# Splitting the tail of a mixture-of-experts decoder by column halves on one Trainium2 core

## The chip, the cores and the metric

The program runs on one core of one Trainium2 chip. The metric is the device time of one execution in microseconds (us), as the median of a few runs. The engines, as the profile names them: PE is TensorE (matrix products, PEld its weight loads), DVE is VectorE, ACT is ScalarE, POOL is GpSimd, SP is SyncE, which issues the DMA transfers here. In the trace each engine's instructions start in the order in which they stand in the program, and an instruction that needs another engine's result waits for it on a semaphore.

## The reference

Two layers of a hybrid decoder work on 256 tokens of 1024 channels in float32. Only the end of the second layer matters here: eight experts, the result added to the residual stream `x`, and the last normalisation.

```
def swiglu(x, w_gate, w_up, w_down):
    return (jax.nn.silu(x @ w_gate) * (x @ w_up)) @ w_down
...
h = rms_norm(x) * (1 + sc2) + sh2
f = moe_ffn(h, ...)          # top 2 of 8 experts for each token, EXPERT_DIM 3584
x = x + g2 * f
...
return rms_norm(x, final_norm_w)   # x * rsqrt(mean(x*x) + EPS) * final_norm_w
```

## The kernel before

The residual stream is a tile `xs` of 128 partitions by two token tiles (t = 0, 1) by 1024 columns, and columns are treated in two halves of 512, called c = 0 and c = 1 here. Weights stream from memory once: SP loads 1 MB pieces into `raw` tiles, and for each half of a piece ACT makes a rounded copy `whi` (line 170) and DVE the rest `wlo = raw - whi` (line 172), so that a product of full precision is three products on PE (`mm3`: high by high, high by low, low by high; every `mm` has line 96). The `whi` and `wlo` tiles go round in a ring of four or five.

The experts run one after the other (`expert`). Each gathers its tokens, makes gate and up products, and then the down products: 14 pieces of `moe_w_down`, each with two blocks of rows (k), and for each block three products into the PSUM tile of c = 0 and three into that of c = 1. In the rows of the order below, `mmt_16767` is the PSUM tile of c = 0 of the last expert and `mmt_16768` that of c = 1; a `whi` and a `wlo` with following numbers are the two parts of one block. After the down products comes `outer` for the expert: DVE scales a half by the token weights and the gate (printed as line 1549, the line of the helper `behind`), ACT makes its rounded part `yh` (also line 1549), DVE the rest `yl`, shown as `sg` (line 1598), PE multiplies both by the transposed selection `PTm` into an `smt` tile for each token tile, and DVE adds it to `xs` (line 1607). For the first seven experts this is queued beside the gate and up products of the next one (`Stages`). After the last expert nothing follows it, so `stages.flush()` issues it at once, and then `finish` runs: ACT squares `xs` and sums it along the columns (`rms_scale`, line 266), DVE turns the sums into 1/sqrt with three Newton steps (`newton`, lines 112 to 123) for each token tile apart, POOL meanwhile multiplies `xs` by the final weight row `fw` (line 1354), and ACT (line 1360) and DVE (line 1358) multiply that by the root and SP writes four blocks of 256 KB to `out` (line 1361). The `overflow` loop behind it is there for experts with more than 128 tokens.

A scheduler places the recorded instructions of each engine. It may move an instruction forward past others that it does not depend on; `tc.issue_after(ins)` (and the helper `behind`, which takes the instruction from the table `last`) keeps what is recorded under it behind `ins` on the engine of `ins`, and nothing else does.

Of the kernel before, what the change touches and what calls it, by code (L numbers as in the profile page):

```python
# [19 lines left out]
P = 128  # L20
D = 1024
# [40 lines left out]
def trunk_kernel(ctx, tc, a, out, dbg=None):  # L62
# [32 lines left out]
    def mm(o, l, r, start, stop):  # L95
        return T.matmul(o, l, r, start=start, stop=stop, skip_group_check=True)  # L96

    def mm3(o, lh, ll, rh, rl, start, stop):
        mm(o, lh, rh, start, False)
        mm(o, lh, rl, False, False)  # L100
        mm(o, ll, rh, False, stop)

    nsm = [0]

# [1205 lines left out]
    def moe(l):  # L1310
        with tc.tile_pool(name=f"mw{l}", bufs=1, reuse_waits="tile", side="right") as xp, \
# [14 lines left out]
            with tc.tile_pool(name=f"mr{l}", bufs=1, reuse_waits="tile") as rp, \  # L1326
# [18 lines left out]
                def finish():  # L1345
# [3 lines left out]
                    o, f = (x.rearrange("p (t n) -> p t n", t=NT) for x in (o, f))  # L1349
                    for t in range(NT):  # L1350
                        rs = rms_scale(t, lambda c: o[:, t, c * 512:(c + 1) * 512])
# [3 lines left out]
                        for c in range(2):  # L1355
                            cs = slice(c * 512, (c + 1) * 512)
                            if c:
                                V.tensor_scalar(o[:, t, cs], f[:, t, cs], rs, None, op0=OP.mult)
                            else:
                                A.activation(o[:, t, cs], f[:, t, cs], AF.Copy, scale=rs)  # L1360
                            nc.sync.dma_start(out[t * P:(t + 1) * P, cs], o[:, t, cs])

                for e in range(NE):
                    x, Pm, i = ready.pop(0)

                    def between():
                        Pm = behind("lo", pair, e + 1)
                        ready.extend((x, Pm, i) for i, x in enumerate(gather(l, ep, h2, Pm, 2)))
                    expert(l, e, ep, xp, x, lambda t, Pm=Pm, i=i: Pm[:, t, i], lambda t, e=e: wsel[:, t, e:e + 1], g2,
                           after_first if e == 0 else None, between if e % 2 and e < NE - 1 else None)  # L1370
                stages.flush()
                finish()
                overflow(l, mp, ep, xp, h2, g2, ovi, ovs, finish)
            extra.clear()

# [175 lines left out]
    def expert(l, e, ep, xp, x, Pm, wsel, g2, after=None, between=None):  # L1551

# [23 lines left out]
        def weights():  # L1576
# [9 lines left out]
            V.tensor_copy(ws, pst[:, 256:257])  # L1586
            return PTm, ws

        def outer(pss):
            yield 2  # L1590
            yp = []
            for c in range(2):
                y = pss[c]
                behind("lo", V.scalar_tensor_tensor, y, y, ws, g2[c], op0=OP.mult, op1=OP.mult)
                yh = ep.tile([P, 512], F32R, name="yh", tag="yh", bufs=2)
                yl = ep.tile([P, 512], F32R, name="sg", tag="sg", bufs=3)
                behind("hi", A.activation, yh, y, AF.Copy)
                V.tensor_sub(yl, y, yh.bitcast(F32))
                yp.append((yh, yl))
            yield 1  # L1600
            for c in range(2):
                cs = slice(c * 512, (c + 1) * 512)
                for t in range(NT):
                    ps = smtile()
                    mm(ps, PTm[:, t * P:(t + 1) * P], yp[c][0], True, False)
                    mm(ps, PTm[:, t * P:(t + 1) * P], yp[c][1], False, True)
                    V.tensor_add(xs[:, t, cs], xs[:, t, cs], ps)

        for c in range(ED // 512):
            pss = []  # L1610
# [12 lines left out]
                PTm, ws = weights()  # L1623
        pss = [mmtile(), mmtile()]
        KE = ED // P
        for k0 in range(0, KE, 2):
            if k0 == KE - 6 and between is not None:
                between()
            hi, lo = chunk(moe_src("moe_w_down", e)[k0 // 2, 0], 2, D)
            for k in range(2):  # L1630
                kk = k0 + k
                o = kk // 4 % 2 * 1024 + kk % 4 * P
                for c in range(2):
                    cs = slice(c * 512, (c + 1) * 512)
                    a2 = act[kk // 8]
                    mm3(pss[c], a2[:, o:o + P], a2[:, o + 512:o + 512 + P], hi[k][:, cs], lo[k][:, cs], kk == 0,
                        kk == KE - 1)
            stages.run()
        stages.add(outer(pss))

    def overflow(l, mp, ep, xp, h2, g2, ovi, ovs, finish):

# [153 lines left out]
```

## Time and profile before

| | us |
|---|---|
| three runs | 1902.97, 1904.64, 1906.03 |
| their median | 1904.64 |
| the profiled execution | 1905.8 |
| its span, from the first to the last instruction | 1904.0 |
| PE busy in that span | 1847.7 |

Times inside the trace count from the start of the span. The profiled execution is 1.2 us over the median, and 1.8 us of it lie outside the span. A busy PE is the sum of its instructions' durations; products overlap, so the distance between starts tells the pace. In a timeline row the columns are the start, the time covered by the merged instructions, engine, line, operation, output and input, the number merged, and in brackets how long the engine was idle before and what ended that.

### The profile page before, as it was taken

Reading aid. Unit: us, or ns where it says so; the run is one execution under the profiler, and the core shown is the slowest. Engines: PE = TensorE matmul, PEld = TensorE weight load, DVE = VectorE, ACT = ScalarE, POOL = GpSimd, SP = SyncE. Lnnn points to the kernel's source line nnn. Section 1 sums busy time; section 2 is a strip of 40 time slices with the busy share of each in tenths; the row PEclk is TensorE's granted clock in tenths of the full one; section 3 lists DMA queues with packets and bytes.
Section 4 is the critical chain, followed back from the end, with each engine's and each line's share of the span. In section 5 each row is a group of like instructions: output and inputs, shape, how many; then the busy total and the mean of one; then the engine's idle time right before and its main releaser. Section 6 shows DMA issues by size and latency. Waiting matters only on the chain.

```text
span 1904.0 us, 25647 instructions
## 1 busy us (share of the span) xinstructions
PE 1847.7 (97%) x9490; PEld 1548.6 (81%) x9490; DVE 1598.7 (84%) x2313; ACT 1230.9 (65%) x1599; POOL 41.5 (2%) x61
## 2 busy tenths in 40 slices
PE   8989999999999999999999999999999999999996
PEld 6889888788879898888888777878878888788785
DVE  7988786876578987667999889998898999899997
ACT  4655445544455644446777787777777777777775
POOL 0000100000000000000000000000000000000001
PEclk9999999999999999999999999999999999999998
DMA  9463545676545555558899989999889999899892
GB/s 364 175 213 125 199 177 202 241 290 238 205 169 199 198 185 193 176 200 329 334 356 343 354 320 361 343 365 355 339 333 356 351 358 368 311 354 381 332 353 91
DMA packets 75016, 530.19 MB, mean 278 GB/s; under 512 B 8578, under 2 KB 8962, under 8 KB 12548
## 3 DMA queue, kind: packets, MB, share of 16 engines
q1 hardware_dynamic: 74884, 528.49, 73.6%
q8 instruction: 76, 1.25, 0.3%
q14 instruction: 56, 0.46, 0.1%
HBM read 527.41 MB, written 1.05 MB: 278 GB/s over the span
## 4 chain that ended last, share of the span: by engine, by line
PE 84%; DVE 8%; ACT 4%; DMA 2%; issue 2%; ACTq 0%; DVEq 0%; SPq 0%
PE mmt L96 74%; PE smt L96 5%; DVE wlo L172 2%; DMA raw<-in_w_in_dram 2%; PE sst L96 2%; PE trt L1566 1%; DVE raw L199 1%; ACT whi L170 1%; DVE cv L588 1%; ACT sg L1527 1%; PE trt L258 0%; PE trt L1073 0%; PE trt L96 0%; DMA raw<-in_ffn_w_up_dram 0%; ACT htmp L289 0%
## 5 line engine op out<-in xcount | busy, mean ns | idle before, releaser
L172 DVE TENSOR_TENSOR wlo<-raw,whi 128x1024 fp32r<-128x1024 f32 (+1 forms) x874 | 1041.9, 1221 | 151.7 <-ACT whi L170 131.6
L170 ACT ACTIVATE whi<-raw 128x1024 fp32r<-128x1024 f32 (+1 forms) x874 | 907.8, 1059 | 316.4 <-PE mmt L96 263.4
L96 PE MATMUL mmt<-whi,xx 128*128 128x512 f32 x1792 | 578.9, 397 | 0.0
L96 PEld LDWEIGHTS mmt<-whi,xx 128*128 128x128 f32 x1792 | 337.4, 188 | 74.9
L96 PE MATMUL mmt<-wlo,xx 128*128 128x512 f32 x896 | 357.6, 399 | 4.9 <-DVE wlo L172 4.9
L96 PE MATMUL mmt<-whi,act 128*128 128x512 f32 x896 | 281.0, 391 | 1.2 <-ACT whi L170 1.2
L96 PEld LDWEIGHTS mmt<-wlo,xx 128*128 128x128 f32 x896 | 168.8, 188 | 52.1 <-DVE wlo L172 16.5
L96 PEld LDWEIGHTS mmt<-whi,act 128*128 128x128 f32 x896 | 167.4, 188 | 36.4 <-ACT whi L170 2.5
L96 PE MATMUL mmt<-whi,hh 128*128 128x512 f32 (+2 forms) x480 | 183.9, 389 | 4.8 <-ACT hh L292 2.0
L96 PE MATMUL mmt<-wlo,hh 128*128 128x512 f32 (+2 forms) x480 | 180.9, 382 | 1.0 <-DVE wlo L172 1.0
L96 PE MATMUL mmt<-whi,hl 128*128 128x512 f32 (+2 forms) x480 | 180.8, 382 | 0.5 <-DVE hl L293 0.5
L96 PE MATMUL mmt<-wlo,act 128*128 128x512 f32 x448 | 175.2, 391 | 1.8 <-DVE wlo L172 1.6
L199 DVE CUSTOM_DVE_ANT_0 raw<-raw,sc_b,pv 128x1024 f32<-128x1024 f32 x96 | 121.7, 1281 | 7.9 <-DMA raw<-in_w_ada_gate_dram 4.7
L96 PEld LDWEIGHTS mmt<-whi,hh 128*128 128x128 f32 x480 | 90.7, 189 | 22.8 <-ACT hh L292 2.6
L96 PEld LDWEIGHTS mmt<-whi,hl 128*128 128x128 f32 x480 | 90.6, 189 | 18.0 <-DVE hl L293 1.0
L96 PEld LDWEIGHTS mmt<-wlo,hh 128*128 128x128 f32 x480 | 90.6, 189 | 17.4 <-DVE wlo L172 1.6
L96 PEld LDWEIGHTS mmt<-wlo,act 128*128 128x128 f32 x448 | 84.1, 188 | 22.3 <-DVE wlo L172 4.4
L96 PE MATMUL mmt<-hh,wlo 128*128 128x256 f32 x320 | 92.9, 292 | 4.4 <-DVE wlo L172 4.4
L96 PE MATMUL mmt<-hh,whi 128*128 128x256 f32 x320 | 93.4, 293 | 1.5 <-ACT whi L170 1.5
L96 PE MATMUL mmt<-hl,whi 128*128 128x256 f32 x320 | 92.1, 289 | 0.0
L1549 ACT ACTIVATE act<-trt 128x512 fp32r<-128x512 f32 x56 | 33.1, 591 | 72.0 <-PE trt L1566 72.0
L96 PEld LDWEIGHTS mmt<-hh,wlo 128*128 128x128 f32 x320 | 61.9, 194 | 6.0 <-DVE wlo L172 5.8
(422 smaller groups left out, 2209.6 us busy)
## 6 DMA issues: line engine op xcount, KB each, us to landing
raw<-in_moe_w_gate_dram SPq DMA_DIRECT2D x112, 1024.0 KB, 5.9
raw<-in_moe_w_up_dram SPq DMA_DIRECT2D x112, 1024.0 KB, 6.4
raw<-in_moe_w_down_dram SPq DMA_DIRECT2D x112, 1024.0 KB, 6.6
raw<-in_w_in_dram SPq DMA_DIRECT2D x50, 1024.0 KB, 4.9
raw<-in_w_ada_pair_dram SPq DMA_DIRECT2D x32, 1024.0 KB, 5.5
raw<-in_w_ada_gate_dram SPq DMA_DIRECT2D x16, 1024.0 KB, 4.9
raw<-in_ffn_w_down_dram SPq DMA_DIRECT2D x11, 1024.0 KB, 4.8
raw<-in_ffn_w_gate_dram SPq DMA_DIRECT2D x10, 1024.0 KB, 4.9
```

What stands on the lines that cost most here:

```text
L96: return T.matmul(o, l, r, start=start, stop=stop, skip_group_check=True)
L170: last["hi"] = A.activation(hi[:, :m], r, AF.Copy)
L172: last["lo"] = V.tensor_sub(lo[:, :m], r, hi[:, :m].bitcast(F32))
L199: last["ada"] = V.tensor_tensor_reduce(r, r, sc_b, 1.0, pv[l][:, PP_BADA + i:PP_BADA + i + 1], OP.mult, OP.add, modc[l][:, i:i + 1])
L588: V.scalar_tensor_tensor(cv[:, s:], o[:, :S - s], tapw(3 - s), cv[:, s:], op0=OP.mult, op1=OP.add)
L1527: A.activation(tmp[:, o], ps[:, o], AF.Identity, scale=sc, bias=sh)
L1549: return trace(*args, **kw)
L1566: last["tr"] = T.transpose(ps[:, b * P:(b + 1) * P], sg[:, b * P:(b + 1) * P], ident)
```

## The change

Three things are changed.

First, the down products of every expert are recorded by a new function `down(k0, c, ...)`, with the loop over c outside that over the two blocks k, where before k was outside.

Second, the last expert is given `finale`. Its last three pieces of down weights are kept in `tail`. They are recorded as: c = 0 of all three pieces, the scaling of c = 0 (`scaled(0)`), c = 1 of the first two, then behind the last of these the two additions of c = 0, their squares and the products with the final weights `f` for c = 0 (on DVE), then c = 1 of the third piece behind the last outer product of c = 0, then behind `f` and the squares the scaling of c = 1, its additions and squares.

Third, `finish` is given these sums. Both token tiles share one chain of Newton steps on tiles of 2 columns, c = 1 of the output is one DVE operation of three factors, c = 0 is ACT's product of `f` and the root. POOL has no products any more.

```
@@ trunk_kernel, moe
                 def finish(early=None):
                     if early is None:
                         fw, o, f = outs()
                         ss = squares(o)
                     else:
                         fw, o, f, ss = early
                     d = small(2, "fd2")
                     V.tensor_scalar(d, ss[:, 0:2], 1.0 / D, EPS, op0=OP.mult, op1=OP.add)
                     V.scalar_tensor_tensor(d, ss[:, 2:4], 1.0 / D, d, op0=OP.mult, op1=OP.add)
                     rs = small(2, "frs2")
                     newton(rs, d)
                     for t in range(NT):
                         for c in range(2):
                             cs = slice(c * 512, (c + 1) * 512)
                             r = rs[:, t:t + 1]
                             if c or early is None:
                                 V.scalar_tensor_tensor(o[:, t, cs], xs[:, t, cs], r, fw[:, cs], op0=OP.mult, op1=OP.mult)
                             else:
                                 A.activation(o[:, t, cs], f[:, t, cs], AF.Copy, scale=r)
                             nc.sync.dma_start(out[t * P:(t + 1) * P, cs], o[:, t, cs])
...
-                            G.tensor_mul(f[:, t, cs], xs[:, t, cs], fw[:, cs])
...
+                def finale(c, add):
...
+                    for t in range(NT):
+                        add(t)
+                        last["square"] = A.activation(o[:, t, cs], xs[:, t, cs], AF.Square,
+                                                      accum_out=ss[:, 2 * c + t:2 * c + t + 1])
+                    if c == 0:
+                        for t in range(NT):
+                            last["f"] = V.tensor_mul(f[:, t, cs], xs[:, t, cs], fw[:, cs])
@@ expert
+        def down(k0, c, hi, lo):
+            for k in range(2):
...
+                last["down"] = mm3(pss[c], a2[:, o:o + P], a2[:, o + 512:o + 512 + P], hi[k][:, cs], lo[k][:, cs], kk == 0,
+                                   kk == KE - 1)
+        tail = []
         for k0 in range(0, KE, 2):
...
+            if k0 >= KE - 6 and finale is not None:
+                tail.append((k0, w))
+                continue
+            for c in range(2):
+                down(k0, c, *w)
             stages.run()
...
+        stages.flush()
+        for k0, w in tail:
+            down(k0, 0, *w)
+        yp = scaled(0, pss)
+        for k0, w in tail[:2]:
+            down(k0, 1, *w)
+        behind("down", finale, 0, lambda t: add(0, t, yp))
+        k0, w = tail[2]
+        behind("outer", down, k0, 1, *w)
+        with tc.issue_after(last["f"].ins), tc.issue_after(last["square"].ins):
+            yp1 = scaled(1, pss)
+        finale(1, lambda t: add(1, t, yp1))
```

`scaled(c)` and `add(c, t, yp)` hold what `outer` held before: the scaling with its two parts, and two outer products with one addition.

Three places show what this does to the order. The first is PE at the end of the last expert, before the change: the six down products of the last block, then the outer products into the `smt` tiles, `yh` and `sg` being the two parts of a scaled half.

```order
L96 MATMUL mmt_16767<-whi_17070,act_16841 128x512
L96 MATMUL mmt_16768<-whi_17070,act_16841 128x512
L96 MATMUL mmt_16767<-wlo_17071,act_16841 128x512
L96 MATMUL mmt_16767<-whi_17070,act_16841 128x512
L96 MATMUL mmt_16768<-wlo_17071,act_16841 128x512
L96 MATMUL mmt_16768<-whi_17070,act_16841 128x512
L96 MATMUL smt_17096<-yh_17087,PTm_16160 128x512
L96 MATMUL smt_17100<-yh_17087,PTm_16160 128x512
L96 MATMUL smt_17104<-yh_17092,PTm_16160 128x512
L96 MATMUL smt_17096<-sg_17088,PTm_16160 128x512
L96 MATMUL smt_17100<-sg_17088,PTm_16160 128x512
```

And PE at the same place in the changed program, where `whi_17036` is a block of the second piece of `tail` and `whi_17042` and `whi_17046` are the two of the third:

```order
L96 MATMUL mmt_16768<-whi_17036,act_16841 128x512
L96 MATMUL mmt_16767<-wlo_17043,act_16841 128x512
L96 MATMUL mmt_16767<-whi_17042,act_16841 128x512
L96 MATMUL mmt_16767<-whi_17046,act_16841 128x512
L96 MATMUL mmt_16767<-wlo_17047,act_16841 128x512
L96 MATMUL mmt_16767<-whi_17046,act_16841 128x512
L96 MATMUL smt_17090<-yh_17069,PTm_16160 128x512
L96 MATMUL smt_17095<-yh_17069,PTm_16160 128x512
L96 MATMUL smt_17090<-sg_17070,PTm_16160 128x512
L96 MATMUL smt_17095<-sg_17070,PTm_16160 128x512
L96 MATMUL mmt_16768<-whi_17042,act_16841 128x512
L96 MATMUL mmt_16768<-wlo_17043,act_16841 128x512
```

The four outer products of c = 0 have moved ahead of six down products of c = 1. The twelve products of c = 1 that the text puts between the scaling and the outer products (those of the first two pieces) stand further up, among the products of c = 0; between the last product of c = 0 and the first outer product there is none.

The second place is DVE at the end, before, from the last `wlo` on (`ssd` and `rsq` are the sums and Newton values of a token tile):

```order
L1598 TENSOR_TENSOR sg_17088<-mmt_16767,yh_17087 128x512
L1598 TENSOR_TENSOR sg_17093<-mmt_16768,yh_17092 128x512
L1607 TENSOR_TENSOR xs_66<-xs_66,smt_17096 128x512
L1607 TENSOR_TENSOR xs_66<-xs_66,smt_17100 128x512
L1607 TENSOR_TENSOR xs_66<-xs_66,smt_17104 128x512
L1607 TENSOR_TENSOR xs_66<-xs_66,smt_17108 128x512
L268 TENSOR_SCALAR ssd_17119<-ss_17116 128x1
```

And DVE there in the changed program (`raw_17087` is `f`, `raw_17085` is `fw`, `fss4` holds the sums):

```order
L1583 SCALAR_TENSOR_TENSOR mmt_16767<-mmt_16767,ws_16162,g2_8540 128x512
L1629 TENSOR_TENSOR sg_17070<-mmt_16767,yh_17069 128x512
L1637 TENSOR_TENSOR xs_66<-xs_66,smt_17090 128x512
L1637 TENSOR_TENSOR xs_66<-xs_66,smt_17095 128x512
L1394 TENSOR_TENSOR raw_17087<-xs_66,raw_17085 128x512 x2
L1583 SCALAR_TENSOR_TENSOR mmt_16768<-mmt_16768,ws_16162,g2_8547 128x512
L1353 TENSOR_SCALAR fd2_17123<-fss4_17089 128x2
L1629 TENSOR_TENSOR sg_17110<-mmt_16768,yh_17109 128x512
L1637 TENSOR_TENSOR xs_66<-xs_66,smt_17113 128x512
L1637 TENSOR_TENSOR xs_66<-xs_66,smt_17118 128x512
L1354 SCALAR_TENSOR_TENSOR fd2_17123<-fss4_17089,fd2_17123 128x2
```

The scaling of c = 1 has moved behind the two additions of c = 0 and the two products with the final weights.

The third place is PE in the middle of an expert's down products, before, one piece (blocks `whi_16934` and `whi_16938`) and its two halves:

```order
L96 MATMUL mmt_16767<-whi_16934,act_16439 128x512
L96 MATMUL mmt_16768<-whi_16934,act_16439 128x512
L96 MATMUL mmt_16767<-wlo_16935,act_16439 128x512
L96 MATMUL mmt_16767<-whi_16934,act_16439 128x512
L96 MATMUL mmt_16768<-wlo_16935,act_16439 128x512
L96 MATMUL mmt_16768<-whi_16934,act_16439 128x512
L96 MATMUL mmt_16767<-whi_16938,act_16439 128x512
L96 MATMUL mmt_16768<-whi_16938,act_16439 128x512
L96 MATMUL mmt_16767<-wlo_16939,act_16439 128x512
```

And the same piece in the changed program:

```order
L96 MATMUL mmt_16767<-whi_16934,act_16439 128x512
L96 MATMUL mmt_16768<-whi_16934,act_16439 128x512
L96 MATMUL mmt_16767<-wlo_16935,act_16439 128x512
L96 MATMUL mmt_16767<-whi_16934,act_16439 128x512
L96 MATMUL mmt_16767<-whi_16938,act_16439 128x512
L96 MATMUL mmt_16768<-wlo_16935,act_16439 128x512
L96 MATMUL mmt_16768<-whi_16934,act_16439 128x512
L96 MATMUL mmt_16768<-whi_16938,act_16439 128x512
L96 MATMUL mmt_16767<-wlo_16939,act_16439 128x512
```

The first product by the second block's `whi` has moved two places forward, the last one by the first block's tiles one place back, and the first one by `wlo` of each block has kept its place. This is so in the down products of all eight experts. On DVE, ACT and SP nothing else is moved; SP issues the load of the final weights and the four output transfers in the same places, the outputs now in the order ACT, DVE, ACT, DVE.

## Rows read from the trace of the kernel before

**Rows 1.** The page: busy time of each engine, and the shares of the chain that ended last.

```profile
PE 1847.7 (97%) x9490; PEld 1548.6 (81%) x9490; DVE 1598.7 (84%) x2313; ACT 1230.9 (65%) x1599; POOL 41.5 (2%) x61
...
PE 84%; DVE 8%; ACT 4%; DMA 2%; issue 2%; ACTq 0%; DVEq 0%; SPq 0%
```

**Rows 2.** The timeline of PE and of DVE's `wlo` over the last down products.

```profile
1859.21 22.32 DVE L172 TENSOR_TENSOR wlo<-raw,whi 128x1024 fp32r<-128x1024 f32 x17
...
1882.86 0.84 PE L96 MATMUL mmt<-whi,act 128*128 128x512 f32 x3
1883.54 0.39 PE L96 MATMUL mmt<-wlo,act 128*128 128x512 f32 x1
1883.76 0.39 PE L96 MATMUL mmt<-whi,act 128*128 128x512 f32 x1
...
1884.22 0.39 PE L96 MATMUL mmt<-whi,act 128*128 128x512 f32 x1
```

**Rows 3.** The timeline behind them, engine by engine (DVE, ACT, PE): the scaling, the outer products, the additions and the squares.

```profile
1884.19 1.42 DVE L1549 SCALAR_TENSOR_TENSOR mmt<-mmt,ws,g 128x512 f32<-128x512 f32 x2 [2.67 <-PE mmt L96]
1885.62 0.69 DVE L1598 TENSOR_TENSOR sg<-mmt,yh 128x512 fp32r<-128x512 f32 x1
1887.06 0.69 DVE L1607 TENSOR_TENSOR xs<-xs,smt 128x512 f32<-128x512 f32 x1
1887.67 1.87 DVE L1607 TENSOR_TENSOR xs<-xs,smt 128x512 f32<-128x512 f32 x3
...
1884.98 1.26 ACT L1549 ACTIVATE yh<-mmt 128x512 fp32r<-128x512 f32 x2 [4.72 <-DVE mmt L1549]
1887.78 0.63 ACT L266 ACTIVATE raw<-xs 128x512 f32<-128x512 f32 x1 [1.54 <-DVE xs L1607]
1889.02 0.61 ACT L266 ACTIVATE raw<-xs 128x512 f32<-128x512 f32 x1
...
1885.63 0.50 PE L96 MATMUL smt<-yh,PTm 128*128 128x512 f32 x1 [1.03 <-ACT yh L1549]
1888.14 0.39 PE L96 MATMUL smt<-sg,PTm 128*128 128x512 f32 x1
```

**Rows 4.** The timeline of POOL's products with the final weights and of DVE's small operations beside and behind them.

```profile
1887.88 4.96 POOL L1354 TENSOR_TENSOR raw<-xs,raw 128x512 f32<-128x512 f32 x4 [968.52 <-DVE xs L1607]
...
1889.76 0.65 DVE L269 SCALAR_TENSOR_TENSOR ssd<-ss,ssd 128x1 f32<-128x1 f32 x1
...
1891.67 1.19 DVE L123 SCALAR_TENSOR_TENSOR rsq_y<-rsq_t,rsq_y 128x1 f32<-128x1 f32 x1
...
1893.15 0.15 DVE L123 SCALAR_TENSOR_TENSOR rsq_y<-rsq_t,rsq_y 128x1 f32<-128x1 f32 x1
```

**Rows 5.** The timeline of the start of the program, where the same chain of Newton steps for two token tiles runs once, on tiles of 2 columns: its second operation, and the first users of the root on DVE and on ACT.

```profile
8.00 0.16 DVE L304 SCALAR_TENSOR_TENSOR ssd<-ss,ssd 128x2 f32<-128x2 f32 x1
...
10.16 0.88 DVE L328 TENSOR_SCALAR xn<-xs,rs 128x512 f32<-128x512 f32 x2
10.23 1.33 ACT L327 ACTIVATE xn<-xs,rs 128x512 f32<-128x512 f32 x2 [2.46 <-DVE rs L123]
```

**Rows 6.** The timeline of the output: the first product with the root on DVE, the last on ACT, the first and the last issue of SP; and the windows of the last microseconds (stretch, its length, busy time of PE, PEld, DVE, ACT and POOL, granted clock, DMA share, GB/s).

```profile
1893.92 0.48 DVE L1358 TENSOR_SCALAR raw<-raw,rs 128x512 f32<-128x512 f32 x1
1895.04 0.72 ACT L1360 ACTIVATE raw<-raw,rs 128x512 f32<-128x512 f32 x1 [0.39 <-DVE rs L123]
1894.43 0.35 SPq L1361 DMA_DIRECT2D out_dram<-raw  x1
1896.21 0.41 SPq L1361 DMA_DIRECT2D out_dram<-raw  x1
...
1895.00:1896.00 1.00, 0.00 (x0) 0.00 (x0) 0.49 (x1) 0.72 (x1) 0.00 (x0) 0.50 0.75 270
1897.00:1898.00 1.00, 0.00 (x0) 0.00 (x0) 0.00 (x0) 0.00 (x0) 0.00 (x0) 0.50 1.02 381
1898.00:1899.00 1.00, 0.00 (x0) 0.00 (x0) 0.00 (x0) 0.00 (x0) 0.00 (x0) 0.50 0.14 45
```

**Rows 7.** A group by form (line, engine, operation, tiles, count, busy time, mean ns of one, idle before): a product of two SBUF tiles of 128x512 on DVE.

```profile
L928 DVE TENSOR_TENSOR tg<-tg 128x512 f32<-128x512 f32 x8 | 5.5, 685 | 0.1
```

**Rows 8.** Windows around the last product of PE, with the columns of rows 6; the granted clock is the third number from the end.

```profile
1889.00:1890.00 1.00, 0.00 (x0) 0.00 (x0) 0.90 (x4) 1.00 (x5) 1.00 (x2) 1.00 0.06 16
1890.00:1891.00 1.00, 0.00 (x0) 0.00 (x0) 0.93 (x4) 0.34 (x2) 1.00 (x2) 0.74 0.00 0
```

**Rows 9.** Waits of PE and of ACT for the weights' ring over the experts, 960 to 1885 us (total, times, longest), and DVE at the change from one expert to the next.

```profile
PE mmt L96 <- DVE wlo L172: 6.5, 10, 0.8
PE mmt L96 <- ACT whi L170: 1.2, 3, 0.4
...
ACT whi L170 <- PE mmt L96: 121.0, 358, 2.7
...
1768.97 1.88 DVE L1607 TENSOR_TENSOR xs<-xs,smt 128x512 f32<-128x512 f32 x3 [0.81 <-PE smt L96]
```

**Rows 10.** The timeline of PE in the dense layer, whose down products stand in runs of three for one PSUM tile: the first and the last of 24 that follow each other.

```profile
494.66 0.39 PE L96 MATMUL mmt<-wlo,ah 128*128 128x512 f32 x1
...
499.87 0.39 PE L96 MATMUL mmt<-whi,ah 128*128 128x512 f32 x1
```

More of the change, by code (lines that the diff above doesn't have):

```diff
@@ L1347, in finish, with outs, squares @@
+                def outs():
                     fw, o, f = (raw_tile() for _ in range(3))
                     nc.sync.dma_start(fw[:, :D], a["final_w"])
-                    o, f = (x.rearrange("p (t n) -> p t n", t=NT) for x in (o, f))
+                    return (fw, *(x.rearrange("p (t n) -> p t n", t=NT) for x in (o, f)))
+                def squares(o):
+                    ss = small(4, "fss4")
                     for t in range(NT):
-                        rs = rms_scale(t, lambda c: o[:, t, c * 512:(c + 1) * 512])
@@ L1352, in finish @@
                         for c in range(2):
                             cs = slice(c * 512, (c + 1) * 512)
-                            G.tensor_mul(f[:, t, cs], xs[:, t, cs], fw[:, cs])
[L1355 to L1361, printed above, removed]
+                            A.activation(o[:, t, cs], xs[:, t, cs], AF.Square, accum_out=ss[:, 2 * c + t:2 * c + t + 1])
@@ new lines, in squares @@
+                    return ss
+                early = []
+                def finale(c, add):
+                    if not early:
+                        early.extend((*outs(), small(4, "fss4")))
+                    fw, o, f, ss = early
+                    cs = slice(c * 512, (c + 1) * 512)
+                    for t in range(NT):
[3 more added lines that the diff above has]
+                    if c == 0:
+                        for t in range(NT):
+                            last["f"] = V.tensor_mul(f[:, t, cs], xs[:, t, cs], fw[:, cs])
@@ L1369, in moe @@
                     expert(l, e, ep, xp, x, lambda t, Pm=Pm, i=i: Pm[:, t, i], lambda t, e=e: wsel[:, t, e:e + 1], g2,
-                           after_first if e == 0 else None, between if e % 2 and e < NE - 1 else None)
+                           after_first if e == 0 else None, between if e % 2 and e < NE - 1 else None,
+                           finale if e == NE - 1 else None)
                 stages.flush()
-                finish()
+                finish(early)
                 overflow(l, mp, ep, xp, h2, g2, ovi, ovs, finish)
@@ L1549, in behind, with expert @@
             return trace(*args, **kw)
-    def expert(l, e, ep, xp, x, Pm, wsel, g2, after=None, between=None):
+    def expert(l, e, ep, xp, x, Pm, wsel, g2, after=None, between=None, finale=None):
         xh, xl = x
@@ L1587, in weights, with scaled, add @@
             return PTm, ws
+        def scaled(c, pss):
+            y = pss[c]
+            behind("lo", V.scalar_tensor_tensor, y, y, ws, g2[c], op0=OP.mult, op1=OP.mult)
+            yh = ep.tile([P, 512], F32R, name="yh", tag="yh", bufs=2)
+            yl = ep.tile([P, 512], F32R, name="sg", tag="sg", bufs=3)
+            behind("hi", A.activation, yh, y, AF.Copy)
+            V.tensor_sub(yl, y, yh.bitcast(F32))
+            return yh, yl
+        def add(c, t, yp):
+            cs = slice(c * 512, (c + 1) * 512)
+            ps = smtile()
+            for i in range(2):
+                last["outer"] = mm(ps, PTm[:, t * P:(t + 1) * P], yp[i], i == 0, i == 1)
+            V.tensor_add(xs[:, t, cs], xs[:, t, cs], ps)
         def outer(pss):
             yield 2
[L1591 to L1599, printed above, removed]
+            yp = [scaled(c, pss) for c in range(2)]
             yield 1
             for c in range(2):
-                cs = slice(c * 512, (c + 1) * 512)
                 for t in range(NT):
[L1604 to L1607, printed above, removed]
+                    add(c, t, yp[c])
         for c in range(ED // 512):
@@ L1628, in expert @@
                 between()
[L1629 to L1637, printed above, removed]
-            stages.run()
-        stages.add(outer(pss))
+            w = chunk(moe_src("moe_w_down", e)[k0 // 2, 0], 2, D)
+            if k0 >= KE - 6 and finale is not None:
+                tail.append((k0, w))
+                continue
+            for c in range(2):
+                down(k0, c, *w)
+            stages.run()
+        if finale is None:
+            stages.add(outer(pss))
+            return
+        stages.flush()
[10 more added lines that the diff above has]
+        finale(1, lambda t: add(1, t, yp1))
     def overflow(l, mp, ep, xp, h2, g2, ovi, ovs, finish):
```

25 lines of the change are left out of this document (23 added, 2 removed).

## The prediction

> **What bounds the kernel now.** I read the page first, then the timeline of the last 45 us, then the waits over the experts. The page says that PE is busy for 1847.7 of 1904.0 us and holds 84% of the chain that ended last [rows 1]: up to the last down product the kernel is as long as PE's products. The timeline shows where that ends. PE starts its last down product at 1884.22, with a start every 0.227 us before it (1882.86 to 1884.22 are six steps) [rows 2]. What follows is a chain with little on PE: scaling on DVE at 1884.19, `yh` on ACT at 1884.98, outer products at 1885.63, the first addition at 1887.06, the last ending near 1889.5, squares on ACT [rows 3], the roots on DVE, the first output issue at 1894.43 and the last at 1896.21 [rows 6]. Some 20 us of the 1904 are this tail, and the change is aimed at it. In the middle of it POOL multiplies for 4.96 us, and beside it DVE's operations on one column take 0.65 and 1.19 us, where the same kind takes 0.15 as soon as POOL is done [rows 4]. A POOL product takes 1.24 there (4.96 over four), so the second to the fourth end at 1890.4, 1891.6 and 1892.8; the two long DVE rows end at 1890.4 and 1892.9. DVE waits for the end of a POOL product.
>
> **The change part by part**, on the clock of the profiled span.
>
> *The earlier half.* Before, c = 0's last product is the one that starts at 1883.76. Now six products of c = 1 are left behind it, and PE has as many down products as before, so it starts six steps before 1884.22: at 1882.86. That is 0.90 earlier. Its `wlo` is there: DVE's last ends at 1881.53 [rows 2]. DVE started scaling 0.43 after that product's start [rows 2, 3]: now 1883.29.
>
> *PE's wait.* The text means twelve products of c = 1 to run while c = 0 is scaled. The order shows them further up, so PE meets the outer products right behind c = 0's last product, and they wait for ACT. From scaling to the first outer product it is 1.44 (1884.19 to 1885.63) [rows 3]: 1884.73, while PE's next start would be 1883.09. PE stands for 1.64 us with six down products behind the waiting instruction, and c = 1 waits for those.
>
> *The first chain.* `yl` starts 1.43 after the scaling (1885.62 to 1884.19) and takes 0.69 [rows 3]; then a product after a wait takes 0.50 as the one at 1885.63 did, and with two hand-overs of 0.04 the addition starts 2.70 after the scaling: 1885.99. (Before it was 2.87, since a product of the other half lay between.) Then DVE has two additions and two products with `fw`. Additions start 0.61 apart (1887.06, 1887.67) [rows 3]; a product of two SBUF tiles takes 0.685 [rows 7] and I give it the same step. Four steps end at 1888.43. ACT's two squares lie beside them and end before. The outer products end PE's wait at 1884.73; the second `sg` product starts near 1885.79, the six down products from 1886.02 to 1887.15, and c = 1 is complete at about 1887.5. So the scaling of c = 1, queued on DVE behind `f`, starts 0.9 after it could.
>
> *The second chain.* It is the first again, with nothing beside it: 1888.43 + 2.70 = 1891.13, second addition 1891.74, its square 0.72 later (1887.06 to 1887.78) at 1892.46, and DVE's use of the sum 0.74 after a square's start (1889.02 to 1889.76) [rows 3, 4]: 1893.20. Before, the additions were all done by 1889.5; now by 1892.4. PE stands still from about 1887.5 until this chain's first outer product, 1888.43 + 1.44 = 1889.87, that is 2.3 us. [...] I let these products run at the full pace, as the window behind the last product did; what the lower level would cost is a rival. [...]
>
> *The roots.* Two token tiles in one chain, without POOL beside it, stand in this trace: from the second operation at 8.00 to the root's user at 10.16, ACT at 10.23 [rows 5]. So 2.16, and ACT's first product starts at 1895.43 and takes 0.72 [rows 6]: 1896.15, SP issues 0.03 later as before (1894.40 to 1894.43): 1896.18. Before, from the use of the first sum to the first issue took 1889.76 to 1894.43, that is 4.67; now 2.98, though three operations stand in each step where two did.
>
> *The output.* The four issues were spread over 1894.43 to 1896.21; now the fourth block is ready at 1895.43 + 1.33 (two ACT products [rows 5]) = 1896.76, and issues 0.43 apart give 1896.18 to 1897.5. That is 1.75 later for the first and 1.3 for the last. The transfers filled the 16 queues at 381 GB/s until just past 1898 [rows 6], 1 MB in 2.8 us, so the first issue sets their end. I take 1.75.
>
> *The down products of the other experts.* The order is changed in all eight. `wlo`'s first use keeps its place, `whi`'s comes two products earlier, and every ring tile is given back one product, 0.227 us, later. In the last stretch the last `wlo` is done at 1881.53 and first used at 1883.54 [rows 2], a lead of 2.0 us, so a later start of ACT and DVE by 0.227 is covered. Where PE waits (10 times for `wlo`, 3 for `whi`, 7.7 us together), the row at the change of experts has DVE itself waiting 0.81 for PE's outer product [rows 9], so there too the ring isn't last. Runs of three into one PSUM tile cost nothing: 24 in the dense layer's order take 494.66 to 499.87, 23 steps of 0.2265 [rows 10]. I take 0; the bounds are +3.0 (0.227 at each of 13 waits) and -0.5 (if an earlier `whi` saved one of its waits of 0.4).
>
> *The sum.* -0.90 for the earlier half; +3.8 because scaling, outer products and additions of the halves now follow each other (from c = 0 ready to the last addition's end 9.2 instead of 5.4 us); about -1.1 for what follows the additions (3.8 to the first issue instead of 4.9). Together +1.75, in the profiled execution 1905.8 to 1907.6 (its 1.8 us outside the span kept). Against the median of the runs, 1904.64, it is 1906.4. A measurement of this kernel can tell about 0.2%, 3.8 us, from no change: this is no change that can be told, on the slow side.
>
> **The rivals.**
>
> *The clock falls in the second gap.* For it speaks that before the change the clock went down between 1890 and 1891, after PE's last product at 1888.53 [rows 8]; against it that it was still full in the window before that, and that the end of the last down product, not a long rest, stands ahead of this gap. At half pace the product that waited takes up to 0.5 more than its 0.50, and the others 0.2 to 0.4 in all. It gives 1906.9 to 1907.3, still no change.
>
> *The ring becomes last: slower.* At the changes of experts and behind the gathers DVE and ACT have work besides `whi` and `wlo`, and there the lead is used up. If at each of the 13 waits PE then stands 0.227 us longer, it is +3.0 on top of the tail: 1909.4, slower by 0.25%. It decides where the lead of `wlo` over PE is below 0.227; in the last stretch it is 2.0, and DVE's own wait for PE [rows 9] speaks against it.
>
> *The cover works after all.* If PE found other products to do while c = 0 is scaled, its 1.64 would go, and c = 1 would be complete at 1885.9 while DVE is at the additions. DVE's queue, not PE, then holds c = 1, so its scaling still starts at 1888.43, and the end stays: 1906.4. Only with c = 0 twelve products earlier, as the text means it, would it gain: then DVE's last `wlo` at 1881.53 is the bound, c = 0 is scaled at about 1882.1, the four steps on DVE end 1.2 earlier than in my sum, and so does all behind them: 1905.2. The order speaks against it: the twelve are not there.
>
> *Faster by over 0.2%* would take 3.8 us, more than the whole gain from POOL and the earlier half together (0.9, and 4.67 less 2.98). I know no mechanism for it here; the chance is for a base that repeats less well than three runs show.
>
> **How the numbers follow.** The forecast as it stands 0.66; with the fallen clock 0.17; the cover working, at 1905.2, 0.04 (all three within 0.2%: 0.87); the ring last 0.10 (slower; 0.01 of it less than the limit, counted with no change: slower 0.09, same 0.88); faster 0.03. The range goes down from 1906.4 by the runs' own spread (1.7 below their median), by 0.5 for the other experts and by 0.45 if the last issue and not the first sets the end: 1903.7. Upwards it takes the spread (1.4) and the clock's 0.9, 1908.7, and a little of the ring's case: 1909.0.
>
> **What would show it.** Right: in the changed profile PE idle for some 1.6 us before the first `yh` product, with six down products of c = 1 behind it; DVE from addition to `f` to the scaling of c = 1 without a gap; small operations of 0.16 us in a chain of 2.2 us; the first output issue 1.5 to 2 us later than 1894.43. The experts' waits of PE near 7.7 us. Wrong: PE's waits in the experts more than 2 us longer, a `mmt` pace other than 0.227, or a last addition that ends before 1891.

## The result, and the profile after

The changed kernel takes 1918.33 us (median of 6 runs, 1917.7 to 1919.5) where the kernel before takes 1905.34 beside it (median of 6): a ratio of 1.007, 95% interval 1.0057 to 1.0083. It is slower by 13 us, and the prediction of 1906.4 with no change that can be told was wrong. The profiled execution of the changed kernel has 1919.07 us and a span of 1917.3, 13.3 more than before.

The page of the changed kernel, busy time of each engine and the chain's shares, answers to [rows 1]:

```profile
PE 1858.7 (97%) x9490; PEld 1547.6 (81%) x9490; DVE 1594.5 (83%) x2308; ACT 1230.3 (64%) x1599; POOL 36.2 (2%) x57
...
PE 83%; DVE 9%; ACT 4%; DMA 2%; issue 2%; SPq 0%; DVEq 0%; ACTq 0%
```

PE has the same 9490 products and is busy 11.0 us longer (1858.7 to 1847.7). A loss in the tail would show as idle time of PE; this is work that takes longer. The waits of PE in the experts, with the columns of [rows 9], are not longer either:

```profile
PE mmt L96 <- DVE wlo L172: 6.5, 10, 0.8
PE mmt L96 <- ACT whi L170: 0.9, 3, 0.3
```

So the next view is the costliest groups of the page (line, engine, operation, output<-moving tile,stationary tile, shape, count, busy time, mean ns of one, idle time before them), four of the kernel before and then the same four of the changed one:

```profile
L96 PE MATMUL mmt<-whi,xx 128*128 128x512 f32 x1792 | 578.9, 397 | 0.0
...
L96 PE MATMUL mmt<-whi,act 128*128 128x512 f32 x896 | 281.0, 391 | 1.2 <-ACT whi L170 1.2
...
L96 PEld LDWEIGHTS mmt<-whi,act 128*128 128x128 f32 x896 | 167.4, 188 | 36.4 <-ACT whi L170 2.5
...
L96 PE MATMUL mmt<-wlo,act 128*128 128x512 f32 x448 | 175.2, 391 | 1.8 <-DVE wlo L172 1.6
```

```profile
L96 PE MATMUL mmt<-whi,xx 128*128 128x512 f32 x1792 | 578.8, 397 | 0.0
...
L96 PE MATMUL mmt<-whi,act 128*128 128x512 f32 x896 | 286.2, 396 | 0.9 <-ACT whi L170 0.9
...
L96 PEld LDWEIGHTS mmt<-whi,act 128*128 128x128 f32 x896 | 167.4, 188 | 41.7 <-ACT whi L170 2.2
...
L96 PE MATMUL mmt<-wlo,act 128*128 128x512 f32 x448 | 177.5, 396 | 1.8 <-DVE wlo L172 1.6
```

The down products (`act`) take 5 ns longer in the mean; the weight loads take 188 ns as before and only stand 5.3 us longer in all, behind the products. The gate and up products (`xx`) already had the longer duration before, and keep it. Five nanoseconds look like nothing, but products follow each other without a gap (behind a down product by `whi` the next one starts 227 ns after it in the kernel before and 233 ns in the changed one, in the median of each trace), and the 11.0 us that PE is busy longer are most of the 13.3 by which the span grows. It is not the order alone, since products that the change does not touch are longer too. The dense layer, 1400 us ahead of the tail, was the prediction's own witness for the pace [rows 10]. The timeline of PE at the same place in the changed kernel, the first and the last of 24:

```profile
494.69 0.39 PE L96 MATMUL mmt<-wlo,ah 128*128 128x512 f32 x1
...
500.06 0.40 PE L96 MATMUL mmt<-whi,ah 128*128 128x512 f32 x1
```

23 steps of 0.2335 us, where they were 0.2265.

The tail itself went as foretold. The timeline of the changed kernel, from c = 0's last product to the first output, answers to [rows 2, 3, 6]:

```profile
1893.52 0.40 PE L96 MATMUL mmt<-whi,act 128*128 128x512 f32 x1
1893.96 0.76 DVE L1583 SCALAR_TENSOR_TENSOR mmt<-mmt,ws,g 128x512 f32<-128x512 f32 x1 [1.65 <-PE mmt L96]
...
1895.40 0.73 PE L96 MATMUL smt<-yh,PTm 128*128 128x512 f32 x2 [1.48 <-ACT yh L1583]
...
1896.66 1.28 DVE L1637 TENSOR_TENSOR xs<-xs,smt 128x512 f32<-128x512 f32 x2 [0.59 <-PE smt L96]
...
1897.87 1.29 DVE L1394 TENSOR_TENSOR raw<-xs,raw 128x512 f32<-128x512 f32 x2
...
1899.07 0.75 DVE L1583 SCALAR_TENSOR_TENSOR mmt<-mmt,ws,g 128x512 f32<-128x512 f32 x1
...
1900.51 1.12 PE L96 MATMUL smt<-yh,PTm 128*128 128x512 f32 x2 [2.26 <-ACT yh L1583]
1901.42 1.05 PE L96 MATMUL smt<-sg,PTm 128*128 128x512 f32 x2
1902.09 1.28 DVE L1637 TENSOR_TENSOR xs<-xs,smt 128x512 f32<-128x512 f32 x2 [0.91 <-PE smt L96]
...
1907.14 2.84 SPq L1365 DMA_DIRECT2D out_dram<-raw  x4
```

DVE's additions, `f` and the scaling of c = 1 follow each other without a gap, PE stands 1.48 us ahead of the first outer product (1.64 foretold) and 2.26 ahead of the second chain's (2.3 foretold). At the end of that second gap the clock fell. Windows of the changed kernel, with the columns of [rows 8]:

```profile
1899.00:1900.00 1.00, 0.00 (x0) 0.00 (x0) 0.89 (x3) 0.14 (x1) 0.00 (x0) 1.00 0.00 0
1900.00:1901.00 1.00, 0.49 (x2) 0.40 (x2) 0.51 (x1) 0.45 (x1) 0.00 (x0) 0.82 0.00 0
1901.00:1902.00 1.00, 1.00 (x4) 0.53 (x2) 0.18 (x1) 0.00 (x0) 0.00 (x0) 0.50 0.00 0
```

The granted clock is full until 1900, 0.82 in the next microsecond and 0.50 behind it. The products there take 1.12 and 1.05 us for two, those of the first chain 0.73.

**What can change a product's duration far from the edit.** In these products `whi` and `wlo`, the parts of the model's weights, are the moving operand (128x512 in the rows); the stationary one (128*128), whose load of 188 ns has a row of its own (PEld, LDWEIGHTS), is `act`, `xx`, `ah`, `yh` or `hh`. The change gives three new names to small tiles (`fss4`, `fd2`, `frs2`). By the addresses in the two built programs that is 192 bytes more per partition in the pool `cp`, and by those addresses `whi`, `wlo`, `hh`, `xx` and `raw`, allocated behind it, move by 192 bytes. The pools that the kernel opens with `side="right"`, with `act`, `ah` and the `yh` of the second mixer's products, stay. So for the products of 512 columns the distance from the moving tile (`whi`, `wlo`) to the stationary one changes for `act`, `ah`, `yh`, and not for `xx` and `hh`. From here a distance is the address of `whi` less that of the stationary tile, modulo 256 bytes. Before: 0 for `act`, `ah`, `yh`, `hh`, and 128 for `xx`. After: 192 for the first three.

### The profile page after: what moved, and what is told of

It reads as the page before. It is cut to its first block, busy times and chain, and to the rows that moved or that the text cites. A ratio compares the mean times of both kernels' runs of the same rounds, so it can differ in the third digit from the quotient of the medians.

```text
span 1917.3 us, 25629 instructions
## 1 busy us (share of the span) xinstructions
PE 1858.7 (97%) x9490; PEld 1547.6 (81%) x9490; DVE 1594.5 (83%) x2308; ACT 1230.3 (64%) x1599; POOL 36.2 (2%) x57
## 3 DMA queue, kind: packets, MB, share of 16 engines
HBM read 527.41 MB, written 1.05 MB: 276 GB/s over the span
## 4 chain that ended last, share of the span: by engine, by line
PE 83%; DVE 9%; ACT 4%; DMA 2%; issue 2%; SPq 0%; DVEq 0%; ACTq 0%
PE mmt L96 73%; PE smt L96 5%; DVE wlo L172 3%; PE sst L96 2%; DVE raw L199 1%; PE trt L1600 1%; ACT whi L170 1%; DMA raw<-in_w_in_dram 1%; DVE cv L588 1%; ACT sg L1561 1%; PE trt L1073 0%; PE trt L258 0%; PE trt L96 0%; DMA raw<-in_w_ada_pair_dram 0%; DMA raw<-in_ffn_w_gate_dram 0%
## 5 line engine op out<-in xcount | busy, mean ns | idle before, releaser
L96 PE MATMUL mmt<-whi,act 128*128 128x512 f32 x896 | 286.2, 396 | 0.9 <-ACT whi L170 0.9
L1583 DVE TENSOR_TENSOR act<-trt,act 128x512 fp32r<-128x512 f32 x56 | 38.6, 689 | 34.2 <-ACT act L1583 33.6
```

## The experiments

**Theory 1**: the distance of the two operands sets the pace of a product. **Theory 2**, the rival nearest to the edit: the new order of the down products does. **Theory 3**: the place of the weights' tiles, or added bytes as such.

**e1, the bytes without the change.** One unused tile in the kernel before:

```diff
             h2 = [mp.tile([P, NT, D], F32R, name="h2", tag="h2", bufs=2) for _ in range(2)]
+            cp.tile([P, 48], F32, name="pad")
```

> The kernel before with one unused tile of 192 bytes per partition in the pool of the last layer, so that whi, wlo, hh, xx and the raw tiles lie 192 bytes further on, as they do in the changed kernel; the order of the work is that of before. Theory 1 (PE's pace hangs on where the two operands of a product lie to each other): the products of whi and wlo with act, ah, al and yh go from 227 to 233 ns apart, page group mmt<-whi,act from 281.0 us towards 286, the time is 10 to 11 us over before, about 1915.5. Theory 2 (the new order of the down products sets the slower pace): pace 227 ns, time that of before within 2 us, about 1905.5.

**e2, the change without the bytes:**

```diff
-                    d = small(2, "fd2")
+                    d = small(2, "ssd2")
-                    rs = small(2, "frs2")
+                    rs = small(2, "rs2")
-                        early.extend((*outs(), small(4, "fss4")))
+                        early.extend((*outs(), small(4, "ss4")))
```

> The changed kernel, its three new small tiles put into small tiles that the program has already, so that no address moves; order, operations and tail are those of the change. Theory 1 (addresses): pace of the down products back at 227 ns, mmt<-whi,act 281 us, time 1907 to 1908, that is the tail's own 2 us over before. Theory 2 (order): pace 233 ns stays, time about 1918.

e1 measured 1915.83 us against 1904.86, ratio 1.0057 (1.0040 to 1.0074); e2 1908.39, ratio 1.0018 (1.0008 to 1.0027). The two groups of down products on the page of e1, and then of e2:

```profile
L96 PE MATMUL mmt<-whi,act 128*128 128x512 f32 x896 | 286.4, 397 | 0.9 <-ACT whi L170 0.9
...
L96 PE MATMUL mmt<-wlo,act 128*128 128x512 f32 x448 | 177.3, 396 | 1.8 <-DVE wlo L172 1.6
```

```profile
L96 PE MATMUL mmt<-whi,act 128*128 128x512 f32 x896 | 281.1, 391 | 1.2 <-ACT whi L170 1.2
...
L96 PE MATMUL mmt<-wlo,act 128*128 128x512 f32 x448 | 175.3, 391 | 1.8 <-DVE wlo L172 1.6
```

An unused tile makes the old kernel as slow on PE as the changed one, and the whole change without it has the old pace. Theory 2 falls: the new order costs nothing on PE, which is busy for 1845.7 us on the page of e2 and for 1847.7 before.

**e3, e5, e10, e11: other numbers of bytes.** The edit of e1 with 512, 256, 32 and 128 bytes.

> As e1_pad192 with an unused tile of 512 bytes per partition. Theory 1, in the form that the distance of the operands modulo 512 bytes counts: distance as before, pace 227 ns, time of before, 1905.5 within 2 us. Theory 3 (the absolute place of the weights' tiles counts, or any shift is harmful): pace 233 ns, about 1915.5. Theory 2 (order): 1905.5.

> As e1_pad192 with an unused tile of 256 bytes per partition: the distance of whi and wlo to act, ah and yh becomes 256 modulo 512. Theory 1 with the modulus 512: pace 232 to 234 ns, time about 1915.5. Theory 1 with the modulus 256 (or a divisor of it): pace 227 ns, time 1905 within 2 us. The gate and up products with xx, whose tile moves along, stay at 232 ns in both.

> The kernel before with 32 unused bytes per partition: whi and wlo lie 32 bytes off a multiple of 256 to act, ah and yh. If any distance but a multiple of 256 costs the same: pace 232 to 234 ns, 1915 to 1916. If the cost grows with the distance: pace between 227 and 230 ns, 1906 to 1911.

> The kernel before with 128 unused bytes per partition: distance of whi and wlo to act, ah and yh 128 from a multiple of 256, as xx has it. Theory 1 with the modulus 256: pace 232 to 234 ns, 1915 to 1916. With a modulus of 128 (which the slow products with xx speak against): 227 ns, 1905.

**e4, the stationary tile moved instead.** In the kernel before, ahead of `xx` in `gather`:

```diff
+        ep.tile([P, 96], F32, name="pad", tag="pad")
```

> The kernel before with an unused tile of 384 bytes per partition ahead of the gathered tokens xx alone, so that the distance of xx to whi and wlo, 128 bytes modulo 512 before, becomes 0; act, ah, yh stay. Theory 1: the gate and up products of the experts with xx go from 232 to 227 ns apart; some 2700 of them give 13 us, time about 1892. Theories 2 and 3: pace 232 ns as before, time 1905.5 within 2 us.

**e9, still more bytes in the changed kernel**, at the place of e1:

```diff
+            cp.tile([P, 16], F32, name="pad")
```

> The changed kernel with 64 unused bytes per partition MORE, so that its own 192 bytes become a shift of 256; nothing else. Theory 1 with the modulus 256: the products with act, ah and yh are back at 227 ns, and the time falls by 10 to 11 us to that of e2_nopad, 1907 to 1909. Theory 3 (any added bytes, or the absolute place, cost): 1918 or more.

The results together; the means are those of the groups `whi,act` and `whi,xx` on each page, the distances from the addresses in the built programs. Each run was measured beside the kernel before, whose median lay between 1904.86 and 1905.57; the ratio and its interval compare the two:

| run | distance to act | mean ns | distance to xx | mean ns | median us | ratio to before |
|---|---|---|---|---|---|---|
| before | 0 | 391 | 128 | 397 | | |
| after | 192 | 396 | 128 | 397 | 1918.33 | 1.0070 |
| e1 | 192 | 397 | 128 | 397 | 1915.83 | 1.0057 |
| e2 | 0 | 391 | 128 | 398 | 1908.39 | 1.0018 |
| e3, +512 | 0 | 391 | 128 | 397 | 1905.10 | 1.0005 (0.9996 to 1.0015) |
| e5, +256 | 0 | 391 | 128 | 398 | 1904.91 | 0.9994 (0.9985 to 1.0004) |
| e10, +32 | 32 | 396 | 128 | 397 | 1916.38 | 1.0056 (1.0041 to 1.0071) |
| e11, +128 | 128 | 396 | 128 | 397 | 1913.90 | 1.0043 (1.0028 to 1.0058) |
| e4 | 0 | 391 | 0 | 393 | 1895.45 | 0.9949 (0.9932 to 0.9965) |
| e9, after +64 | 0 | 391 | 128 | 398 | 1907.41 | 1.0012 (1.0003 to 1.0021) |

The group `whi,act` on the pages of e5, e10, e11 and e9, one fence each:

```profile
L96 PE MATMUL mmt<-whi,act 128*128 128x512 f32 x896 | 280.9, 391 | 1.2 <-ACT whi L170 1.2
```

```profile
L96 PE MATMUL mmt<-whi,act 128*128 128x512 f32 x896 | 285.7, 396 | 0.9 <-ACT whi L170 0.9
```

```profile
L96 PE MATMUL mmt<-whi,act 128*128 128x512 f32 x896 | 285.5, 396 | 0.9 <-ACT whi L170 0.9
```

```profile
L96 PE MATMUL mmt<-whi,act 128*128 128x512 f32 x896 | 281.1, 391 | 1.2 <-ACT whi L170 1.2
```

In these runs Theory 1 holds with the modulus 256, not the 512 that I had put first: e5, with 391 ns at 256 bytes, decides between the two. A distance of 32 gives the 396 ns of 128 and the 396 or 397 of 192, so of those tried there is 0 and there is the rest, and nothing in between. Theory 3 falls: e9 has more bytes than the changed kernel and is faster, and e3 and e5 shift the same tiles without a loss. The changed kernel has a control of its own: `hl`, the second part of `hh`, moves by the same 192 bytes as `whi`, its distance stays 0, and its products keep their length. Their group before and after:

```profile
L96 PE MATMUL mmt<-whi,hl 128*128 128x512 f32 x424 | 166.5, 393 | 0.5 <-DVE hl L293 0.5
```

```profile
L96 PE MATMUL mmt<-whi,hl 128*128 128x512 f32 x424 | 166.5, 393 | 0.5 <-DVE hl L293 0.5
```

The mean of 393 takes in longer steps from other causes; the median step of this group is 227 ns in both traces. In e4 the weights stay where they are and `xx` moves, and it is the products with `xx` that get shorter. The groups of `xx` on the page of e4:

```profile
L96 PE MATMUL mmt<-whi,xx 128*128 128x512 f32 x1792 | 571.6, 393 | 0.0
...
L96 PE MATMUL mmt<-wlo,xx 128*128 128x512 f32 x896 | 353.9, 395 | 4.9 <-DVE wlo L172 4.9
```

I had expected 13 us from them and 9.4 came. Durations of 393 and 395 are not yet 391: of the steps behind products with `xx`, 8% are 228 ns or less before and 69% in e4 (88% behind `act`), and the rest keeps a longer step though the distance is 0. So the distance is not the only cause of a longer step; what the other is stays open.

The other runs are on the tail, whose cost e2 and e9 show by themselves: 3.5 and 2.3 us over before by medians (1.8 foretold; the intervals reach from 0.6 to 5.1).

**e6, the third part of the change alone** (no POOL products, one chain of roots), in the kernel before:

```diff
-                            G.tensor_mul(f[:, t, cs], xs[:, t, cs], fw[:, cs])
...
+                    newton(rs, d)
...
+                            V.scalar_tensor_tensor(o[:, t, cs], xs[:, t, cs], rs[:, t:t + 1], fw[:, cs], op0=OP.mult, op1=OP.mult)
```

> The kernel before with the third part of the change alone: squares of both token tiles, one chain of Newton steps on 2 columns, no products on POOL, and the output as four DVE operations of three factors; tiles that exist already, no address moves, expert as before. By the prediction's working: sums used at about 1889.8, roots 2.2 later at 1892.0, first issue about 1.7 earlier than before, the last product ends 2.8 after 1892.0; 1903 to 1903.5. Rival (POOL's products hid something that DVE now has to do, or the last issue sets the end): 1904.5 to 1905.5, no gain.

It took 1905.96 against 1905.57, ratio 1.0002 (0.9989 to 1.0015): no gain that can be told, as the rival had it. The timeline of e6, its last down product, DVE's use of the last sum, and the output:

```profile
1882.85 0.39 PE L96 MATMUL mmt<-whi,act 128*128 128x512 f32 x1
...
1889.01 0.16 DVE L1357 SCALAR_TENSOR_TENSOR ssd<-ss,ssd 128x2 f32<-128x2 f32 x1 [0.75 <-ACTq L1647]
...
1891.18 2.74 DVE L1363 SCALAR_TENSOR_TENSOR raw<-xs,rs,raw 128x512 f32<-128x512 f32 x4
1891.96 2.32 SPq L1364 DMA_DIRECT2D out_dram<-raw  x4
```

From the last down product to the first issue it is 9.11 us, before 10.21 [rows 2, 6]: 1.10 less, not the 1.7 that I expected. The sums are used 6.16 after that product, before 5.54 (1889.76 less 1884.22) [rows 2, 4], since one chain for both token tiles begins with the last square and not with the first tile's. To the end of the span it is 19.05 against 19.78, by the spans of the two pages, a gain of 0.7 in the trace that the runs don't resolve.

**e7 and e8, a cover that is there.** e2 with only two pieces split, and six products of c = 1 held behind the twelve of c = 0; e8 moreover without the two `f` ahead of the scaling of c = 1:

```diff
-            if k0 >= KE - 6 and finale is not None:
+            if k0 >= KE - 4 and finale is not None:
...
-        for k0, w in tail[:2]:
-            down(k0, 1, *w)
+        k0, w = tail[0]
+        behind("down", down, k0, 1, *w)
```

> e2_nopad with the cover that the change's text means: only the last two pieces are split, all twelve products of c = 0 come first, then six of c = 1 (held behind them) while c = 0 is scaled, then its outer products, then the last six of c = 1. By the prediction's rival on the cover: PE's wait of 1.5 us ahead of the first outer product goes to below 0.3, c = 0 is scaled 1.4 us earlier and the end comes about 1.2 us earlier than in e2_nopad, about 1907.2, still over before, since DVE takes the two halves one after the other. Rival (the lack of cover is what costs the tail): 1905 or less.

> e7_cover without the two products f ahead of the scaling of c = 1 on DVE; all four output blocks are DVE operations of three factors instead. By the prediction's working the scaling of c = 1 starts 1.3 us earlier, the last output product 0.7 later in its row of four: about 1906.2. Rival (f isn't on the path, PE's last six products are): 1907.2 or more.

e7 took 1907.85, ratio 1.0003 (0.9994 to 1.0013), e8 1905.50, ratio 1.0002 (0.9992 to 1.0011). Both intervals take in no change, and they overlap, so what follows rests on the traces, one of each run. The timeline of e8:

```profile
1879.92 0.62 PE L96 MATMUL mmt<-whi,act 128*128 128x512 f32 x2
1880.68 0.50 PE L96 MATMUL mmt<-wlo,act 128*128 128x512 f32 x1
1881.02 0.64 PE L96 MATMUL mmt<-whi,act 128*128 128x512 f32 x2
1881.46 0.76 DVE L1580 SCALAR_TENSOR_TENSOR mmt<-mmt,ws,g 128x512 f32<-128x512 f32 x1 [0.83 <-PE mmt L96]
...
1882.90 0.73 PE L96 MATMUL smt<-yh,PTm 128*128 128x512 f32 x2
...
1885.79 0.76 DVE L1580 SCALAR_TENSOR_TENSOR mmt<-mmt,ws,g 128x512 f32<-128x512 f32 x1 [0.33 <-PE mmt L96]
...
1893.52 2.70 SPq L1365 DMA_DIRECT2D out_dram<-raw  x4
```

The first outer product follows without a wait: the cover works. From the last product of c = 0 (1881.02) to the first issue it is 12.50 us, in e2 13.30 (below), and that product stands six steps earlier in PE's work. Yet, against PE's work, e8 only draws level with the kernel before. PE lost 0.41 waiting for a `wlo` here (from the second product of the row at 1879.92, which starts at 1880.15, two steps took 0.87 where 0.454 is usual). Twelve products of c = 1 are left behind the one at 1881.02, so without that wait and in one row the last down product would start at 1881.02 - 0.41 + 12 x 0.227 = 1883.33. From there it is 10.19 to the first issue, before 10.21.

**e12, what the experiments point to**: the kernel before with 128 bytes ahead of `xx` and the tail of e6.

```diff
+        ep.tile([P, 32], F32, name="pad", tag="pad")
```

> The kernel before with 128 unused bytes per partition ahead of xx (distance of xx to whi and wlo 256 modulo 512 in place of 128), and with the squares, roots and output of e6_no_pool. Theory 1 with the modulus 256: gate and up products near 229 ns as in e4_xx384, -9.4 us, and the shorter tail, -0.7: 1894 to 1895. If multiples of 512 count for xx: 1904.

It took 1892.54 us against 1905.07, ratio 0.9937 (0.9921 to 0.9952), the lowest median of all. That is 1.5 below the 1894 that was foretold, and the interval (1890.0 to 1895.9) takes 1894 in. Its page has `whi,xx` at the length of e4, with 128 bytes where that had 384, as the modulus 256 wants it:

```profile
L96 PE MATMUL mmt<-whi,xx 128*128 128x512 f32 x1792 | 571.7, 394 | 0.0
```

Against e4 (0.9949) the tail of e6 is within the intervals.

## Why the prediction was wrong

The step that failed is "The down products of the other experts", where "I take 0" for a reordered loop, with bounds of +3.0 and -0.5 from the ring's waits alone. The waits were right (6.5 and 0.9 us in the changed kernel) and so was the remark that runs of three into one PSUM tile cost nothing (391 ns in e2, as before). What was not weighed is that the change allocates: 192 bytes moved the weights against the stationary tiles, and 1344 products with `act` (896 and 448) and 528 with `ah`, `yh` and their second parts `al`, `yl` took some 5 to 6 ns more each. 1872 by 5.5 ns is 10.3 us; e1 measured 11.0. With the tail's 2.3 to 3.5 us (e9, e2) that is the 13. The prediction named "a `mmt` pace other than 0.227" as what would show it wrong, and that is what the trace shows; but none of its rivals had a cause for it, so no bound of the range did. The trace of before held the sign: products of one shape with two durations, 391 with `act` and 397 with `xx`, in one program.

Term by term the tail was right in sum. From c = 0's last product to the first issue the working had 13.32 us (1882.86 to 1896.18). The timeline of e2, where no address moved:

```profile
1883.42 0.39 PE L96 MATMUL mmt<-whi,act 128*128 128x512 f32 x1
...
1890.39 0.73 PE L96 MATMUL smt<-yh,PTm 128*128 128x512 f32 x2 [2.26 <-ACT yh L1583]
...
1891.66 1.28 DVE L1637 TENSOR_TENSOR xs<-xs,smt 128x512 f32<-128x512 f32 x2 [0.60 <-PE smt L96]
...
1896.72 2.50 SPq L1365 DMA_DIRECT2D out_dram<-raw  x4
```

It is 13.30, and 3.78 of it behind the last addition (3.8 foretold). In the changed kernel it is 13.62.

- *The clock in the second gap*, a rival at 0.5 to 0.9: it fell in the changed kernel and cost 0.3 (from the scaling of c = 1 to its first addition 3.02 us, 1899.07 to 1902.09, in e2 2.71). In e7 it fell too (gap 2.27, granted clock 0.90 and then 0.50). In e2, behind a gap of the same 2.26 us, it stayed at 1.00 through these products and was 0.50 only behind them, from 1892 on. What decides it is open; either way it is 0.3 of the 13 us.
- *The ring becomes last*: did not happen; the waits are those of before.
- *The cover*: priced at 1.2 us. e7 has it, and its c = 0 was ready 0.95 earlier (six steps of 0.227 less 0.41 of waiting for `wlo`), but its clock fell too and its outer pairs took 0.4 longer, which leaves 0.5 in the trace; the intervals of e7 and e2 overlap, so the runs don't show it. That DVE's queue holds c = 1, as the rival argued, e8 shows: without `f` ahead of the scaling of c = 1 the first issue comes 0.8 sooner behind c = 0. Then PE holds it: the wait of 0.33 us before the scaling at 1885.79 ends with a down product.
- *Faster by over 0.2%* was given 0.03, for want of a mechanism. There is one, not in this change but in the same cause taken the other way: e4 and e12.

The runs show that the addresses count: 391 against 396 ns, switched by 32 bytes of distance (e10). By what way they do, no run here shows. That the place of the next product's stationary tile counts too, the change from down products to the next expert's gate products suggests: in the trace the last product with `act` and the load of `xx` start together. That product and the load, before and then in e4:

```profile
1760.63 0.40 PE L96 MATMUL mmt<-whi,act 128*128 128x512 f32 x1
1760.63 0.19 PEld L96 LDWEIGHTS mmt<-whi,xx 128*128 128x128 f32 x1
```

```profile
1751.69 0.39 PE L96 MATMUL mmt<-whi,act 128*128 128x512 f32 x1
1751.70 0.19 PEld L96 LDWEIGHTS mmt<-whi,xx 128*128 128x128 f32 x1
```

Its own distance is 0 in both kernels, that of `xx` 128 before and 0 in e4. At the seven such changes the step is 232 to 235 ns before; in e4 it is 226 or 227 at five and 231 at two. In the changed kernel, where its own distance is 192 and that of `xx` 128, the step is 228 to 231 ns, so these two distances alone do not set it. Whether a product's own stationary tile counts as well is not shown.

## What to carry to other kernels

When a kernel is bound by PE, read the mean duration of products of one shape by their tiles before anything else: two values at one shape may be time to be had, and here one unused tile was worth 9.4 us (e4), more than any rewriting of the tail. A mean takes in other delays too (the `hl` group has 393 at distance 0), so compare the median distance between starts as well. A change that allocates, even three tiles of a few columns, can move every tile behind it; compare addresses before looking for the cause in the order of the work, and test by padding the old kernel and by unpadding the new one. And splitting a serial tail into halves helps only as far as the engine that both halves pass through is free: here DVE took the halves one after the other and gave back what the earlier start had won (from c = 0's last product to the first issue 13.30 us in e2, before 10.67 [rows 2, 6]).

## What the runs showed of the hardware that was not expected

By the addresses in the built programs, and in this case's runs, the float32 products with a moving tile of 128x512 are shorter where the moving tile's address and the stationary tile's differ by a multiple of 256 bytes per partition (0, 256 and 512 were tried). The mean of the group `whi,act` is 391 ns at such distances (before, e2, e3, e5, e9) and 396 or 397 at 32, 128 and 192 bytes beyond one (e10, e11; the changed kernel, e1), that of `whi,xx` 397 at 128 bytes before and 393 at 0 in e4; the mean of the `whi,act` weight loads is 188 ns before and in the changed kernel. From start to start the median behind `act` is 227 ns in the trace of before, and 233 (`whi`) and 234 (`wlo`) in that of the changed kernel; behind `xx`, 128 bytes off, it is 232 in both. On this kernel that is 11 us for 1872 products (e1). The granted clock fell behind a gap of 2.26 us in the changed kernel (0.82, then 0.50) and did not in e2 (1.00), with a gap of the same length and the same instructions at other addresses.
